# The third page of an expert's up weights, split ahead of the evacuation of the down rows

## The chip, the cores and the metric

The kernel runs on one core of one Trainium2 chip. The metric is the device time of one execution in microseconds (us); the kernel before was timed three times. Where a span of the profile is named, it is one execution under the hardware profiler, from its first to its last instruction.

## The reference, cut to what matters

The program is a decoder trunk of two layers on 1024 tokens of width 1024 (16 learned tokens stand in front). Each layer has a mixer, a layer norm, and a mixture of 32 experts of which every token uses two. All numbers are float32. For one expert, with `xb` the rows of the tokens that chose it:

```python
hb = jax.nn.silu(xb @ w_gate[e]) * (xb @ w_up[e])   # w_gate, w_up: 1024 x 512
return hb @ w_down[e]                                # w_down: 512 x 1024
```

The rows that come out are scaled by the token's gate and added to the token's row.

## The kernel before

**Pages.** The kernel keeps weights and larger tiles in 46 pages, each 128 partitions by 1040 floats. A page of weights is 512 KB. One expert needs twelve: four of gate, four of up (256 rows of the matrix each) and four of down (128 rows each). They come in the fixed order gate of expert e, down of expert e-1, up of expert e, and so on; `load_next` (L128) issues the DMA of the next page on SyncE's queue, and `pump` (L149) issues as many as the count of live pages allows.

**Splitting.** TensorE multiplies in fp32r, so each float32 operand becomes a high and a low part, and each product is three matmuls: high by high, low by high, high by low. `split` (L82 to L84) makes the two parts: ScalarE (ACT) copies the page to the high part `whi` (L83), and then VectorE (DVE) subtracts that from the page, which gives the low part `wlo` (L84). `need(i, ahead)` (L153) splits, in the fixed order, all pages up to the `ahead`-th after page `i` that are not yet split. Both parts stand in pages that a used pair has left, so a copy can wait for the last matmul that read the old pair.

**The loop over experts** (`moe`, L586 to L696). Each engine runs its instructions in the order in which this code is written. One pass, for expert e:

1. gate product of e, pages 0 to 2 (`gb`, L610 to L612);
2. the four transposes of the hidden rows of e-1 (`hpose`, tile `htr`, split to `hp`);
3. gate product, page 3;
4. down product of e-1 (`down`, tile `yb`, L644): four pages, six matmuls each, in the order `whi` four times and `wlo` twice;
5. still in `down`: ACT evacuates the two banks of `yb` into `yout`, scaled (L655), and POOL adds the rows to the output in DRAM with an indirect DMA (L657, the scatter);
6. `xpose(e + 1)`: eight transposes of the next expert's tokens (tile `tr`, L329), which ACT copies to `xh` (L83) and DVE subtracts to `xl` (L84); then POOL gathers the tokens of e+3 (L593);
7. up product of e (`ub`, L610 to L612): four pages, six matmuls each;
8. `act`: SiLU of `gb` on ACT and its product with `ub` on DVE (tile `hb`, L622 and L623).

The look-ahead is two pages (`LEAD = 2`). So the last page of down asks for the first two pages of up, and these are split before step 5. The third page of up is first asked for at step 7, by the first page of up; its copy and subtraction therefore stand behind the instructions of steps 5 and 6 on ACT and DVE.

Of the kernel before, what the change touches and what calls it, by code (L numbers as in the profile page):

```python
# [21 lines left out]
T = S + NM  # L22
KD = D // 128
NG = 4
NE = 32
# [21 lines left out]
def hybrid(ctx, tc, x, meta_tokens, lru_w_in, lru_conv_w, lru_conv_b, lru_w_a, lru_b_a, lru_w_i, lru_b_i,  # L47
# [25 lines left out]
    def free(*ts):  # L73
        live[0] -= len(ts)
# [14 lines left out]

    # ------------------------------------------------------------------ weights, in the order of their use  # L90
    items = []
# [68 lines left out]

    # ------------------------------------------------------------------ constants
    ident = cst.tile([128, 128], F32, name="ident")
# [116 lines left out]

    # ------------------------------------------------------------------ layer norm of token rows  # L280
    lnp = {}
# [32 lines left out]
    def skew(n, stages):  # L314
        """tasks: stage after stage for n tiles, each tile a step behind the one before"""
        return [(lambda st=st, i=t - st: stages[st](i)) for t in range(n + len(stages) - 1)
                for st in reversed(range(len(stages))) if 0 <= t - st < n]

    # ------------------------------------------------------------------ routing of a group of tiles
    macc = {}  # L320

    def transposes(src):
        """two banks with src^T, four blocks of 128 columns each"""
        bks = []
        for a in range(2):
            bk = bank("tr")
            for i in range(4):
                k = 4 * a + i
                PE.transpose(bk[:, 128 * i:128 * i + 128], src[:, 128 * k:128 * k + 128], ident)  # L329
            bks.append(bk)  # L330
        return bks
# [6 lines left out]
    def scr(shape, name, dt=F32, bufs=1):  # L338
        """small tile of the routing, in the buffer that the experts' rows take later"""
        n = math.prod(shape) * (2 if dt == BF else 4) // 4  # L340
        if name not in scr_at:
            scr_at[name] = (scr_top[0], n)
            scr_top[0] += n * bufs
        o, w = scr_at[name]
        assert n <= w and scr_top[0] <= D
        i = scr_n[name] = (scr_n.get(name, -1) + 1) % bufs
        ap = yout[:, o + i * w:o + i * w + n]
        if dt != F32:
            ap = ap.bitcast(dt)
        dims = "abc"[:len(shape)]  # L350
        return ap.rearrange(f"p ({' '.join(dims)}) -> p {' '.join(dims)}", **dict(zip(dims, shape)))
# [9 lines left out]
    def route_pick(l, m, pos, tiles, nrm, st):  # L361
# [22 lines left out]
        def gate_steps():  # L384
            # gates: softmax probability of the group times the softmax over the two experts
            V.tensor_scalar(rg, tg, -1.0, 1.0, op0=OP.mult, op1=OP.add)
            yield
            V.reciprocal(rg, rg)
            yield
            V.scalar_tensor_tensor(tg, tg, 1.0, rg, op0=OP.add, op1=OP.mult)  # L390
            yield
            V.tensor_reduce(sg, tg, axis=AX.X, op=OP.add)
            yield
            V.reciprocal(sg, sg)
            yield
# [45 lines left out]
    def route_send(l, m, pos, tiles, st, early, mid, late):  # L441
        # slots: rank among the tokens of the expert
        oh, ix, M = st["oh"], st["ix"], st["M"]
# [47 lines left out]

    # ------------------------------------------------------------------ experts with more than a level of tokens
    def overflow_list(l):
        """the expert and the table column of the j-th block past the first level (row j), and how many there are"""
        ps = bank("cnt")
# [88 lines left out]

    # ------------------------------------------------------------------ mixture of experts
    def moe(l, rows, comb):  # L586
# [48 lines left out]
        def down(e):  # L635
            hp = HB.pop(e)
            hh, hl = hp[:, :F], hp[:, F:2 * F]
            yb = [bank("yb") for _ in range(2)]
            for q in range(KF):
                it = need(down_it[l, e][q], min(LEAD, down_it[l, NE - 1][3] - down_it[l, e][q]))  # L640
                sl = slice(128 * q, 128 * q + 128)
                for st, w in ((hh, "h"), (hl, "h"), (hh, "l")):
                    for a in range(2):
                        PE.matmul(yb[a], st[:, sl], it[w][:, 0, 512 * a:512 * a + 512],  # L644
                                  start=q == 0 and st is hh and w == "h", stop=q == KF - 1 and w == "l")
                drop(down_it[l, e][q])
                pump(room)
            free(hp)
            if e == NE - 1:
                comb["rows"](yb)  # L650
                if not comb["rest"]:
                    return
            y = yout
            for a in range(2):
                A.activation(y[:, 512 * a:512 * a + 512], yb[a], AF.Copy, scale=tab[:, e, 2:3])  # L655
            P.memset(spacer, 0.0)
            P.indirect_dma_start(out=hsum[l], out_offset=bass.IndirectOffsetOnAxis(ap=tv[:, e, 0:1], axis=0),  # L657
                                 in_=y[:, :D], in_offset=None, bounds_check=rows - 1, oob_is_err=False,
                                 compute_op=OP.add)
            if e == NE - 1:  # L660
                comb["load"](comb["rest"])
# [35 lines left out]

    # ------------------------------------------------------------------ projection to the stream, norm, routing
    def nrow(j):
        return 2 if j == META else 128  # L700

    def router(l):
        """the norm's scale and shift move into the router's weights and bias; column sums for its mean"""
        n = NG + NE
# [20 lines left out]
    def out_proj(l, gp, its, resid, cuts, last_chunk, upto):  # L725
        """gp[j]: page of the mixer's rows of tile j, channels on partitions; resid(j, page) loads the stream's rows;
        cuts: columns that are there at the start and after each series of steps that last_chunk returns"""
        UNIT = 0.22
# [67 lines left out]
        def slots(q0, i):  # L796
            """the slot of expert 0 that each token of a tile takes, one column a slot"""
            H = scr([128], "H", BF)
# [62 lines left out]
        for bi, tiles in enumerate(BLOCKS[l]):  # L861
            last = bi == nb_ - 1
            for j in tiles:
                ys[j] = [bank("wo") for _ in range(2)]
            # the last tile takes the low parts first, then one half of the columns after the other
            for a, k in [(a, k) for a in (("l", 0, 1) if last else ("",)) for k in range(KD)]:
# [63 lines left out]

    # ------------------------------------------------------------------ norm after the experts
    def combine(l, order, seq):
        """steps for a tile: h + y / ALPHA, the last expert's rows by products; its statistics; its norm, that of
        ALPHA * h + y"""
        st, yp, oh = {}, [], []
# [75 lines left out]
        def affine(j, dst):  # L1011
            """norm, scale and shift, a half of the columns after the other"""
            for h in range(2):
# [10 lines left out]

    # ================================================================== layer 0: gated linear recurrence
    GRP = [(0, 272), (272, 656), (656, 1040)]
# [32 lines left out]
    def softplus():  # L1059
# [4 lines left out]
        P.tensor_tensor(w2, ecst, w1, op=OP.pow)  # L1064
        # log(1 + z) = 2 atanh(z / (2 + z))
        V.tensor_scalar(w1, w2, 2.0, None, op0=OP.add)
# [7 lines left out]
        V.tensor_tensor(w3, w3, w1, op=OP.mult)  # L1074
        # softplus(-lam) = max(-lam, 0) + 2 atanh(..)
        V.tensor_scalar(w1, lam, -1.0, 0.0, op0=OP.mult, op1=OP.max)
# [53 lines left out]
    def lru_decay(c, r, sp, d, q):  # L1130
        # r = (1 + th) / 2, so -log(a) = 4 softplus(-lam) (1 + th); t = tanh(-log(a) / 2)
        A.activation(d[:, :T], r[:, :T], AF.Exp, bias=sp[1][:, c:c + 1], scale=sp[1][:, c:c + 1])
        A.activation(r[:, :T], r[:, :T], AF.Tanh, bias=sp[0][:, c:c + 1], scale=sp[0][:, c:c + 1])
        # 1 / (1 + t) by a Newton step from (1 + exp(log(a))) / 2; a = 1 - 2t/(1+t), 1 - a^2 = 4t/(1+t)^2
        V.tensor_scalar(d[:, :T], d[:, :T], 0.5, 0.5, op0=OP.mult, op1=OP.add)
# [30 lines left out]
    gp = {}  # L1166
# [101 lines left out]

    # ================================================================== layer 1: gated short convolution
    GRP = [(0, 258), (258, 642), (642, 1026)]  # L1270
# [6 lines left out]
    def h_group(g, ws, bks):  # L1277
        """transposed tiles, a block of 128 columns after the other, with the products that they enter"""
        lo_, hi_ = GRP[g]
# [190 lines left out]
```

## Time and profile before

| | us |
|---|---|
| median of three runs | 2108.13 |
| lowest and highest run | 2107.02, 2109.2 |
| span of the profiled execution | 2108.8 |
| TensorE (PE), matmuls busy | 1980.4 |
| VectorE (DVE) busy | 1618.9 |
| ScalarE (ACT) busy | 1288.5 |
| GpSimd (POOL) busy | 508.3 |

The two loops over experts stand at about 420 to 1010 us and 1460 to 2055 us of the span. Times in the rows are us from the start of the span. PE is the matmuls, PEld the weight loads; SPq is SyncE's queue, which issues the loads of weights. A matmul's record is longer than the distance to the next one, since they are pipelined: the pace is the distance between starts.

### The profile page before, as it was taken

The page shows a single profiled execution, that of the slowest core. Times are in us where ns is not written, and L with a number is a line of the kernel's source. Part 1 is how long each engine was busy: PE and PEld are TensorE (multiplying, and loading weights), DVE is VectorE, ACT ScalarE, POOL GpSimd, SP SyncE. Part 2 cuts the span into 40 slices and gives each one's busy share as a digit, 9 for nine tenths or more (in the row PEclk, how much of TensorE's full clock was granted, in tenths as well). Part 3 has the DMA queues.
Part 4 walks back from the last instruction along what each step waited for, and adds up shares of the span by engine and source line. Part 5 has one row for each costly group of instructions (what it writes and reads, how often), then busy time and mean ns, then how long its engine had stood idle before and what let it go on. Part 6 is the DMA issues. An engine that isn't in the chain of part 4 may idle for free. (4 is left out here: it accounts for less than half of the span.)

```text
span 2108.8 us, 28578 instructions
## 1 busy us (share of the span) xinstructions
PE 1980.4 (94%) x10022; PEld 1677.2 (80%) x10022; DVE 1618.9 (77%) x2089; ACT 1288.5 (61%) x1640; POOL 508.3 (24%) x456
## 2 busy tenths in 40 slices
PE   8999979599999999999889999995999999999996
PEld 7999867477777877777689999873877787777773
DVE  5888875688888898888682223456898889888887
ACT  4666632288888888887630102222788888888872
POOL 3100346412221112220280001365122111222204
PEclk9999989799999999999899999997999999999998
DMA  5211455699999999996533110566999999999954
GB/s 145 57 48 41 150 190 169 248 339 357 364 352 358 353 349 352 352 357 230 166 114 106 41 51 1 200 216 239 327 360 370 368 358 361 364 356 338 365 176 185
DMA packets 255447, 520.40 MB, mean 247 GB/s; under 512 B 26755, under 2 KB 68143, under 8 KB 255300
## 3 DMA queue, kind: packets, MB, share of 16 engines
q1 hardware_dynamic: 229716, 465.31, 61.2%
q0 software_dynamic: 25584, 53.23, 8.9%
q8 instruction: 80, 1.31, 0.2%
q14 instruction: 67, 0.55, 0.1%
HBM read 492.39 MB, written 59.46 MB: 262 GB/s over the span
## 5 line engine op out<-in xcount | busy, mean ns | idle before, releaser
L84 DVE TENSOR_TENSOR wlo<-wraw,whi 128x1024 fp32r<-128x1024 f32 x810 | 955.1, 1229 | 86.8 <-ACT whi L83 74.2
L83 ACT ACTIVATE whi<-wraw 128x1024 fp32r<-128x1024 f32 x824 | 839.1, 1061 | 105.3 <-PE gb L611 34.5
L657 POOL DMA_INDIRECT hs<-yout,tab x63 | 100.0, 1587 | 935.2 <-ACT yout L655 935.2
L644 PE MATMUL yb<-whi,hp 128*128 128x512 f32 x1024 | 281.4, 396 | 1.4 <-ACT hp L83 1.4
L644 PEld LDWEIGHTS yb<-whi,hp 128*128 128x128 f32 x1024 | 193.2, 189 | 47.3 <-ACT hp L83 1.9
L612 PE MATMUL ub<-wlo,xh 128*128 128x512 f32 x512 | 208.1, 407 | 11.4 <-DVE wlo L84 11.2
L610 PE MATMUL gb<-whi,xh 128*128 128x512 f32 x512 | 207.7, 406 | 0.0
L610 PE MATMUL ub<-whi,xh 128*128 128x512 f32 x512 | 206.6, 403 | 0.0
L612 PE MATMUL gb<-wlo,xh 128*128 128x512 f32 x512 | 202.3, 395 | 2.1 <-DVE wlo L84 2.1
L611 PE MATMUL gb<-whi,xl 128*128 128x512 f32 x512 | 202.4, 395 | 0.0
L611 PE MATMUL ub<-whi,xl 128*128 128x512 f32 x512 | 201.8, 394 | 0.0
L644 PE MATMUL yb<-wlo,hp 128*128 128x512 f32 x512 | 160.9, 395 | 0.0
L84 DVE TENSOR_TENSOR xl<-tr,xh 128x512 fp32r<-128x512 f32 x128 | 82.7, 686 | 81.4 <-ACT xh L83 81.4
L612 PEld LDWEIGHTS ub<-wlo,xh 128*128 128x128 f32 x512 | 96.1, 188 | 58.0 <-DVE wlo L84 38.4
L1321 ACT ACTIVATE v<-ip 128x384 f32<-128x384 f32 (+1 forms) x24 | 9.6, 456 | 208.5 <-PE ip L1049 197.6
L84 POOL TENSOR_TENSOR wlo<-wraw,whi 128x1024 fp32r<-128x1024 f32 x14 | 39.8, 2858 | 401.6 <-ACT whi L83 401.6
L593 POOL DMA_INDIRECT xg<-hd,tab x62 | 111.3, 1795 | 38.9 <-issue 16.8
L612 PEld LDWEIGHTS gb<-wlo,xh 128*128 128x128 f32 x512 | 96.5, 188 | 25.6 <-DVE wlo L84 3.4
L644 PEld LDWEIGHTS yb<-wlo,hp 128*128 128x128 f32 x512 | 97.2, 190 | 22.8
L611 PEld LDWEIGHTS gb<-whi,xl 128*128 128x128 f32 x512 | 96.7, 189 | 20.5 <-DVE xl L84 0.9
L610 PEld LDWEIGHTS gb<-whi,xh 128*128 128x128 f32 x512 | 96.8, 189 | 20.0 <-ACT xh L83 0.5
L611 PEld LDWEIGHTS ub<-whi,xl 128*128 128x128 f32 x512 | 96.4, 188 | 19.8
(276 smaller groups left out, 3532.8 us busy)
## 6 DMA issues: line engine op xcount, KB each, us to landing
wraw<-in_moe_w_gate_dram SPq DMA_DIRECT2D x256, 512.0 KB
wraw<-in_moe_w_up_dram SPq DMA_DIRECT2D x256, 512.0 KB
wraw<-in_moe_w_down_dram SPq DMA_DIRECT2D x256, 512.0 KB
wraw<-in_sc_w_in_dram SPq DMA_DIRECT2D x24, 512.0 KB
wraw<-in_lru_w_in_dram SPq DMA_DIRECT2D x16, 512.0 KB
hy<-hs SPq DMA_DIRECT2D x16, 512.0 KB
hd<-res POOLq DMA_DIRECT2D x14, 512.0 KB
hs<-res POOLq DMA_DIRECT2D x12, 512.0 KB
```

Source lines behind the costliest of these rows:

```text
L83: A.activation(hi, src, AF.Copy)
L84: eng.tensor_tensor(lo, src, f(hi), op=OP.subtract)
L593: P.indirect_dma_start(out=xg[e % 2], out_offset=None, in_=hdr[l], in_offset=bass.IndirectOffsetOnAxis(ap=tv[:, e, 0:1], axis=0), bounds_c ...
L610: PE.matmul(bk, xh[:, sl], it["h"][:, k], start=kk == 0, stop=False)
L611: PE.matmul(bk, xl[:, sl], it["h"][:, k], start=False, stop=False)
L612: PE.matmul(bk, xh[:, sl], it["l"][:, k], start=False, stop=kk == KD - 1)
L644: PE.matmul(yb[a], st[:, sl], it[w][:, 0, 512 * a:512 * a + 512], start=q == 0 and st is hh and w == "h", stop=q == KF - 1 and w == "l")
L657: P.indirect_dma_start(out=hsum[l], out_offset=bass.IndirectOffsetOnAxis(ap=tv[:, e, 0:1], axis=0), in_=y[:, :D], in_offset=None, bounds_c ...
L1321: A.activation(zt[c][:, a:b], bk[:, :b - a], AF.Copy)
```

## The change

Two lines are added in `down`, between the last matmul of the down product and the evacuation:

```diff
                 drop(down_it[l, e][q])
                 pump(room)
             free(hp)
+            if e + 1 < NE:
+                need(up_it[l, e + 1][2], 0)
             if e == NE - 1:
                 comb["rows"](yb)
```

Here `e` is the expert of the down product, so `e + 1` is the expert whose up product follows. The rest of the diff takes comments out. On TensorE, SyncE and POOL the instructions stand in the same order as before.

On ACT, in one pass of the first layer: `wraw_5903` and `wraw_5951` are the first and second page of up, `wraw_5963` the third, `wraw_5975` the fourth, `wraw_5991` and `wraw_5993` the next expert's first gate pages. Before:

```order
L83 ACTIVATE whi_6445<-wraw_5951 128x1024
L655 ACTIVATE yout_99<-yb_6407,tab_121 128x512
L655 ACTIVATE yout_99<-yb_6408,tab_121 128x512
L83 ACTIVATE xh_6463<-tr_6465 128x512
L83 ACTIVATE xh_6463<-tr_6470 128x512
L83 ACTIVATE whi_6483<-wraw_5963 128x1024
L83 ACTIVATE whi_6493<-wraw_5975 128x1024
```

And of the changed kernel, at the same place:

```order
L83 ACTIVATE whi_6445<-wraw_5951 128x1024
L83 ACTIVATE whi_6457<-wraw_5963 128x1024
L657 ACTIVATE yout_99<-yb_6407,tab_121 128x512
L657 ACTIVATE yout_99<-yb_6408,tab_121 128x512
L83 ACTIVATE xh_6467<-tr_6469 128x512
L83 ACTIVATE xh_6467<-tr_6474 128x512
L83 ACTIVATE whi_6493<-wraw_5975 128x1024
```

The third page's copy has moved from behind the four instructions of steps 5 and 6 to ahead of them; the fourth page's copy stands where it stood.

On DVE, in the same pass, before:

```order
L84 TENSOR_TENSOR wlo_6446<-wraw_5951,whi_6445 128x1024
L84 TENSOR_TENSOR xl_6464<-tr_6465,xh_6463 128x512
L84 TENSOR_TENSOR xl_6464<-tr_6470,xh_6463 128x512
L84 TENSOR_TENSOR wlo_6484<-wraw_5963,whi_6483 128x1024
L84 TENSOR_TENSOR wlo_6494<-wraw_5975,whi_6493 128x1024
```

And of the changed kernel:

```order
L84 TENSOR_TENSOR wlo_6446<-wraw_5951,whi_6445 128x1024
L84 TENSOR_TENSOR wlo_6458<-wraw_5963,whi_6457 128x1024
L84 TENSOR_TENSOR xl_6468<-tr_6469,xh_6467 128x512
L84 TENSOR_TENSOR xl_6468<-tr_6474,xh_6467 128x512
L84 TENSOR_TENSOR wlo_6494<-wraw_5975,whi_6493 128x1024
```

The subtraction of the third page has moved ahead of the two of the next tokens. The move on ACT stands at 62 places of the program (31 passes in each layer), that on DVE at 60, since the last pass of a layer has no next tokens.

## Rows read from the trace of the kernel before

**Rows 1.** Busy time by stretch, about one pass of the loop; columns first.

```profile
core 0: us, PE busy (x) PEld busy (x) DVE busy (x) ACT busy (x) POOL busy (x), PEclk, DMA share, GB/s
700.00:718.44 18.44, 18.26 (x87) 14.67 (x85) 16.56 (x16) 15.25 (x19) 3.60 (x3) 1.00 1.00 355
```

**Rows 2.** Waits of TensorE over the span: total, times, longest.

```profile
PE ub L612 <- DVE wlo L84: 11.2, 60, 0.2
```

**Rows 3.** Timeline of TensorE, one pass: start, duration, line, idle before.

```profile
714.79 1.09 PE L644 MATMUL yb<-whi,hp 128*128 128x512 f32 x4
...
716.18 1.09 PE L644 MATMUL yb<-whi,hp 128*128 128x512 f32 x4
717.11 0.62 PE L644 MATMUL yb<-wlo,hp 128*128 128x512 f32 x2
...
718.36 0.48 PE L610 MATMUL ub<-whi,xh 128*128 128x512 f32 x1
...
722.04 0.50 PE L612 MATMUL ub<-wlo,xh 128*128 128x512 f32 x1 [0.18 <-DVE wlo L84]
...
724.23 0.39 PE L612 MATMUL ub<-wlo,xh 128*128 128x512 f32 x1
```

**Rows 4.** Timeline of TensorE, the first expert's up product.

```profile
423.14 0.47 PE L610 MATMUL ub<-whi,xh 128*128 128x512 f32 x1
...
426.46 0.39 PE L612 MATMUL ub<-wlo,xh 128*128 128x512 f32 x1
...
427.85 0.39 PE L612 MATMUL ub<-wlo,xh 128*128 128x512 f32 x1
...
428.55 0.39 PE L612 MATMUL ub<-wlo,xh 128*128 128x512 f32 x1
```

**Rows 5.** Timeline of ACT in the pass of rows 3.

```profile
715.92 1.06 ACT L83 ACTIVATE whi<-wraw 128x1024 fp32r<-128x1024 f32 x1 [0.33 <-PE yb L644]
717.54 1.26 ACT L655 ACTIVATE yout<-yb,tab 128x512 f32<-128x512 f32 x2 [0.56 <-PE yb L644]
718.70 1.08 ACT L83 ACTIVATE xh<-tr 128x512 fp32r<-128x512 f32 x2
719.65 2.97 ACT L83 ACTIVATE whi<-wraw 128x1024 fp32r<-128x1024 f32 x3
```

**Rows 6.** Timeline of DVE in the same pass.

```profile
712.38 5.85 DVE L84 TENSOR_TENSOR wlo<-wraw,whi 128x1024 fp32r<-128x1024 f32 x5 [0.25 <-ACT whi L83]
719.33 1.29 DVE L84 TENSOR_TENSOR xl<-tr,xh 128x512 fp32r<-128x512 f32 x2 [1.09 <-ACT xh L83]
720.76 4.63 DVE L84 TENSOR_TENSOR wlo<-wraw,whi 128x1024 fp32r<-128x1024 f32 x4
725.31 0.68 DVE L623 TENSOR_TENSOR hb<-hb,ub 128x512 f32<-128x512 f32 x1
725.91 1.22 DVE L84 TENSOR_TENSOR wlo<-wraw,whi 128x1024 fp32r<-128x1024 f32 x1
```

**Rows 7.** Timeline of POOL, two passes.

```profile
700.63 1.59 POOL L657 DMA_INDIRECT hs<-yout,tab  x1 [14.55 <-ACT yout L655]
...
719.09 1.58 POOL L657 DMA_INDIRECT hs<-yout,tab  x1 [14.55 <-ACT yout L655]
720.97 1.92 POOL L593 DMA_INDIRECT xg<-hd,tab  x1 [0.31 <-issue]
```

**Rows 8.** Waits of ACT for a load, first layer's loop: total, times, longest.

```profile
ACT whi L83 <- DMA wraw<-in_moe_w_gate_dram: 0.3, 1, 0.3
```

**Rows 9.** Timeline of SyncE's queue, last loads of the first layer's experts.

```profile
967.72 4.11 SPq L133 DMA_DIRECT2D wraw<-in_moe_w_down_dram  x4
```

**Rows 10.** Busy time by stretch behind these loads, columns as in rows 1.

```profile
970.00:975.00 5.00, 5.00 (x23) 4.11 (x22) 4.67 (x6) 4.83 (x6) 0.00 (x0) 1.00 0.96 371
975.00:980.00 5.00, 5.00 (x27) 4.16 (x27) 3.72 (x5) 3.81 (x6) 1.61 (x2) 1.00 0.40 135
```

**Rows 11.** Timeline of ACT, last copies of the first layer's experts.

```profile
1003.35 4.84 ACT L83 ACTIVATE whi<-wraw 128x1024 fp32r<-128x1024 f32 x5
```

## The prediction

> **What bounds the kernel now.** I read the busy time by stretch first. In a pass of the loop over experts TensorE (PE) is busy 18.26 of 18.44 us at the full granted clock (1.00, that is 2.4 GHz), while DVE has 16.56 and ACT 15.25 [rows 1]. So PE sets the pace of the pass, and only what lets it stop is worth time. The scatter, once a pass, comes every 719.09 - 700.63 = 18.46 us [rows 7]. The DMA share in the same stretch is 1.00 [rows 1], which makes the loads a second candidate; I come back to it among the rivals.
>
> Next the waits of PE. In the loop there is one that repeats: the up product's low-part matmul (L612) waits for DVE's `wlo`, 60 times, 11.2 us in all [rows 2]. That total is the idle time between records whose ends are modelled, so I measure what it costs by starts instead. The first expert of a layer has no down product before its up product, and its 24 matmuls run without a stop: the 15th starts 426.46 - 423.14 = 3.32 us after the first, the 21st 4.71, the last 5.41 [rows 4]. In the pass of rows 3 the 15th, which is the first to read the third page's low part, starts 722.04 - 718.36 = 3.68 after the first, so 0.36 late, and the last 5.87 after it, so 0.46 late. The stop costs 0.46 us a pass: 0.36 of waiting and 0.10 lost on starting again.
>
> Then the timelines of ACT and DVE, to see why the low part is late. ACT evacuates the down rows from 717.54, copies the next tokens from 718.70, and only at 719.65 begins the third page [rows 5]. DVE stands idle for 1.09 us until the tokens' copy is there, does the two subtractions, and starts the third page's at 720.76 [rows 6]; the matmul starts 1.28 later, at 722.04 [rows 3].
>
> **The change, part by part.** It adds and removes no instruction; it moves one copy on ACT (62 places) and one subtraction on DVE (60 places) ahead of the evacuation and the tokens. PE, SyncE and POOL keep their order, and no load is issued earlier or later in any queue.
>
> *When the third page's copy starts.* It needs two free pages. In the kernel before, the second page's copy waits for PE: it starts at 715.92 [rows 5], 0.04 after the four `whi` matmuls of the last but one down page (714.79 + 1.09 = 715.88) [rows 3]. The next copy in the order takes the pair freed next, that of the last down page, whose `whi` matmuls end at 716.18 + 1.09 = 717.27; so it starts at 717.31. From below: ACT itself is free at 715.92 + 1.06 = 716.98. From above: the whole down product ends at 717.11 + 0.62 = 717.73. I take 717.31, which follows the nearest row.
>
> *What ACT then does.* Copies in a row follow each other by (2.97 - 1.06) / 2 = 0.955 [rows 5], so the evacuation starts at 718.27, 0.73 later than now. The tokens follow after 718.70 - 717.54 = 1.16, at 719.43, and the fourth page after another 0.95, at 720.38.
>
> *What DVE does.* A subtraction starts 720.76 - 719.65 = 1.11 after its copy [rows 5, 6]. The third page's runs from 718.42, when DVE is free (712.38 + 5.85 = 718.23), to 719.64 (1.22 each): in the time in which DVE idles now. The matmul could use it at 718.42 + 1.28 = 719.70 and wants it at 718.36 + 3.32 = 721.68, so it is 2 us early. The tokens' subtractions start 0.63 after their copy as now (719.33 - 718.70), at 720.06, and end at 721.35.
>
> *What is late next.* The fourth page: subtraction at 720.38 + 1.11 = 721.49, usable at 722.77, wanted by the 21st matmul at 718.36 + 4.71 = 723.07. That is 0.30 early. With the copy's bounds above it is 0.63 early or 0.12 late. Behind it DVE goes on without a gap, 1.14 a page ((4.63 - 1.22) / 3): first gate page 722.63, second 723.77, the product `hb` 724.91, third gate page 0.60 later at 725.51 and usable at 726.79. PE, 0.46 earlier than now, starts the next gate product at 724.00 and wants that page 14 steps of 0.233 later, at 727.26: 0.47 early. None of the later pages is tighter, since four transposes and ACT's own waits for PE come between.
>
> *What the moved work holds up.* The evacuation is 0.73 later and the scatter behind it too; POOL is idle for 14.55 us before each scatter [rows 7], so nothing queues there. The copied tokens are first read by the next gate product at 724.0, over 2 us after 721.35. The two banks of the down rows come free 0.73 later, when PE is in the middle of the up product and takes no new bank. I cost these at nothing.
>
> *Sum.* 60 passes by 0.46 us = 27.6 us. The last pass of each layer has no tokens to copy and only a shorter stop; I leave it out. From the profiled span of 2108.8 that gives 2081.2. The median of the runs shown is 0.7 below that span, so I predict 2080.5.
>
> **The rivals.**
>
> *A. The wait moves to the fourth page.* Its reserve of 0.30 is the smallest in the sum. With the copy at its upper bound the matmul is 0.12 late and pays 0.10 for starting again: 0.22 of the 0.46 come back, 13.2 us in 60 passes, and the time is about 2094. At 0.36 late nothing is gained. Against it: the second page's copy starts, in the kernel before, with the last `whi` matmul of the pair that it takes over, and not with the end of a product [rows 3, 5].
>
> *B. The loads cannot follow.* The DMA share is 1.00 at 355 GB/s [rows 1]; a pass of 17.98 us would want 355 x 18.46 / 17.98 = 364. If that can't be had, PE lives on the stock of pages loaded ahead. Over a layer it would draw 30 x 0.46 = 13.8 us more from it. The stock at the end can be read: the last four down pages are issued from 967.72 to 971.83 [rows 9], and the DMA share falls from 0.96 to 0.40 between 970 and 980 [rows 10], so all have landed before 980. The last two of them are copied from 1003.35 on [rows 11], 23 us later. 13.8 fit into 23, and ACT waited for a load once, 0.3 us [rows 8]. Were the stock empty, the time would stay at 2108.
>
> *C. Slower: the gather comes to stand against the fourth page's subtraction.* POOL's queue slides by 0.73: the gather runs from 721.70 to 723.62 instead of from 720.97 [rows 7], and the fourth page's subtraction is now its neighbour. If DVE had to wait until the gather is done, the fourth page would be usable at 723.62 + 1.28 = 724.90, 1.83 late, a pass would lose 1.93 in place of 0.46, and 60 passes 88 us: about 2196. It decides as soon as the subtraction starts later than 721.49 + 0.30 + 0.36 = 722.15. Against it: now the gather runs from 720.97 to 722.89 beside the first two of four subtractions, which take 4.63 / 4 = 1.16 each, and the five with no POOL beside them take 5.85 / 5 = 1.17 [rows 6, 7]. By the Trainium skill (SBUF — State Buffer, section "SBUF: two separate sides") GpSimd and a VectorE operation with two SBUF inputs can lock each other out of a shared port for a whole instruction; the rows just named show no such lock for this pair of instructions, so I give the rule little.
>
> *D. Another wait takes the whole place*, 0.36 or more, of a kind that these rows do not show: no change, 2108.
>
> **How the numbers follow.** The forecast 0.76, A 0.10, B 0.06, D 0.03, C 0.05. About 0.2% (4.2 us) is what a measurement of this kernel can tell from no change. The forecast, A and half of B are faster by more than that: 0.89; D and the other half of B are the same: 0.06; C is slower: 0.05. The forecast's own range is 2077 to 2085: 0.05 us a pass either way in the cost of the stop, and the run-to-run spread. The range runs on upward to take in A's worked case: 2077 to 2096.
>
> **What would show it.** In the changed kernel's waits of PE the line of the up product for `wlo` is gone or a few entries long. In the timeline the last matmul of an up product starts 5.4 us after its first, not 5.87, and scatters follow each other by 18.0 us. On ACT the copy of the third page starts about 0.2 before the down product ends, and the evacuation starts about 0.7 after it. DVE's idle 1.09 us before the tokens shrinks to about 0.4. A wait at the 21st matmul would be A; waits of ACT's copies for loads late in a layer would be B; subtractions of over 1.3 us beside the gather would be C. The prediction is wrong if the stop at the 15th matmul goes and the pass is still over 18.3 us long.

## The result, and the profile after

| | before | after |
|---|---|---|
| median of the runs, us | 2108.66 (2107.02 to 2110.83, 4 runs) | 2077.29 (2075.48 to 2079.23, 4 runs) |
| span of the profiled execution | 2108.8 | 2073.7 |
| start of the first up product of layer 1 | 423.14 | 418.99 |
| from there to the start of the last up product of layer 2 | 1629.77 | 1601.30 |
| from there to the end of the span | 55.9 | 53.4 |

The changed kernel takes 0.9853 of the time before (95% interval 0.9841 to 0.9865): 31.4 us less, where 27.6 were forecast. That is inside the range of 2077 to 2096, but by 0.3 us only. The wait of [rows 2] is gone: this is all that the up and gate products wait for in the whole span. Columns are total, times, longest.

```profile
PE gb L612 <- DVE wlo L84: 1.2, 2, 0.8
```

By stretch, the pass that answers to [rows 1] is 17.98 us long, as is the one behind it, and TensorE (PE) is busy in all of it.

```profile
core 0: us, PE busy (x) PEld busy (x) DVE busy (x) ACT busy (x) POOL busy (x), PEclk, DMA share, GB/s
689.37:707.35 17.98, 17.98 (x88) 14.77 (x86) 16.60 (x16) 15.32 (x20) 3.59 (x3) 1.00 0.99 351
707.35:725.33 17.98, 17.98 (x88) 14.79 (x86) 16.60 (x17) 15.32 (x20) 3.59 (x3) 1.00 0.97 349
```

The timeline of PE in the second of these passes, the first row being the `whi` matmuls of the last but one down page:

```profile
703.80 1.08 PE L644 MATMUL yb<-whi,hp 128*128 128x512 f32 x4
...
705.17 1.09 PE L644 MATMUL yb<-whi,hp 128*128 128x512 f32 x4
706.10 0.62 PE L644 MATMUL yb<-wlo,hp 128*128 128x512 f32 x2
707.35 0.48 PE L610 MATMUL ub<-whi,xh 128*128 128x512 f32 x1
...
710.65 0.39 PE L612 MATMUL ub<-wlo,xh 128*128 128x512 f32 x1
...
712.04 0.40 PE L612 MATMUL ub<-wlo,xh 128*128 128x512 f32 x1
...
712.74 0.39 PE L612 MATMUL ub<-wlo,xh 128*128 128x512 f32 x1
712.97 0.40 PE L610 MATMUL gb<-whi,xh 128*128 128x512 f32 x1
```

The 15th matmul of the up product starts 3.30 us after the first, the 21st 4.69 and the last 5.39: the figures of the undisturbed product of [rows 4] (3.32, 4.71, 5.41) and not those of [rows 3]. ACT and DVE in the same pass answer to [rows 5, 6]:

```profile
704.91 1.07 ACT L83 ACTIVATE whi<-wraw 128x1024 fp32r<-128x1024 f32 x1 [0.33 <-PE yb L644]
706.29 1.06 ACT L83 ACTIVATE whi<-wraw 128x1024 fp32r<-128x1024 f32 x1 [0.31 <-PE yb L644]
707.26 1.25 ACT L657 ACTIVATE yout<-yb,tab 128x512 f32<-128x512 f32 x2
708.40 1.09 ACT L83 ACTIVATE xh<-tr 128x512 fp32r<-128x512 f32 x2
709.36 2.02 ACT L83 ACTIVATE whi<-wraw 128x1024 fp32r<-128x1024 f32 x2
```

```profile
701.44 7.17 DVE L84 TENSOR_TENSOR wlo<-wraw,whi 128x1024 fp32r<-128x1024 f32 x6 [0.26 <-ACT whi L83]
709.03 1.29 DVE L84 TENSOR_TENSOR xl<-tr,xh 128x512 fp32r<-128x512 f32 x2 [0.42 <-ACT xh L83]
710.47 3.50 DVE L84 TENSOR_TENSOR wlo<-wraw,whi 128x1024 fp32r<-128x1024 f32 x3
713.88 0.68 DVE L623 TENSOR_TENSOR hb<-hb,ub 128x512 f32<-128x512 f32 x1
```

The third page's copy is the one at 706.29. Its subtraction is the sixth of the group that begins at 701.44 (before there were five), and stands in what was DVE's idle time, of which 0.42 is left. The group at 710.47 begins with the fourth page.

### The profile page after: what moved, and what is told of

It reads as the page before. It is cut to its first block, busy times and chain, and to the rows that moved or that the text cites. A ratio compares the mean times of both kernels' runs of the same rounds, so it can differ in the third digit from the quotient of the medians.

```text
span 2073.7 us, 28630 instructions
## 1 busy us (share of the span) xinstructions
PE 1958.9 (94%) x10022; PEld 1677.6 (81%) x10022; DVE 1623.4 (78%) x2089; ACT 1289.0 (62%) x1640; POOL 510.4 (25%) x456
## 5 line engine op out<-in xcount | busy, mean ns | idle before, releaser
L612 PE MATMUL ub<-wlo,xh 128*128 128x512 f32 x512 | 201.4, 393 | 0.0
L610 PEld LDWEIGHTS ub<-whi,xh 128*128 128x128 f32 x512 | 96.3, 188 | 19.7
```

Of the source, the lines that this page charges most:

```text
L610: PE.matmul(bk, xh[:, sl], it["h"][:, k], start=kk == 0, stop=False)
L612: PE.matmul(bk, xh[:, sl], it["l"][:, k], start=False, stop=kk == KD - 1)
```

## The experiments

### What belongs to the change: the same programs again, and marked

Both kernels ran once more, and each again with one needless instruction on POOL, in the second layer only, and so later in the program than all that stands ahead of the first loop:

```diff
             P.memset(spacer, 0.0)
+            if l == 1:
+                P.memset(spacer, 0.0)
             P.indirect_dma_start(out=hsum[l], ...
```

> The changed kernel once more, unchanged. My theory: all of the change's gain is 0.46 us in each of the passes of the two loops over experts (about 28 us), and the 4.15 us by which the profiled run was ahead before the first pass began is the scatter of that unchanged part from run to run. Expected: 2077 us (2075 to 2080), up product 5.4 us long, passes 18.0 us, and a first up product that starts anywhere between 418 and 424 us of the span. Rival: the change also shortens the part before the loops; then the first up product starts at about 419 us again and in every kernel that holds the change.

> The kernel before once more, under the profiler, to see whether the 4 us by which the changed kernel is ahead at the start of the first expert's up product (418.99 against 423.14) belong to the kernel or to the single execution. Theory 1, it belongs to the program as a whole (it repeats when the same program runs again, but is set by something that shifts with any edit): first up product at 422.8 to 423.5, first to last up product 1629.8 within 0.5, time 2108. Rival, it varies from one execution to the next: anywhere from 418 to 424. Rival, the change itself gives the 4 us: 423.1 too, so this run alone does not tell it from theory 1; the next two do.

> The kernel before with one needless instruction added: in the second layer POOL clears its one-element spacer twice ahead of each scatter instead of once (0.09 us on an engine that idles 14.5 us there). Up to the second layer the program is word for word the same. Theory 1: the loops stay at 5.87 us an up product and 1629.8 within 1 from first to last, while the first up product can start anywhere from 418 to 424 and not at 423.1; time 2103 to 2110. Rival, what stands ahead of the loops decides by itself: 423.1 within 0.4 again.

> The changed kernel with the same needless instruction on POOL in the second layer. Theory 1: up products 5.41 us, 1601.3 within 0.6 from first to last, the first at anywhere from 418 to 424; time 2073 to 2081. Rival, the change itself makes the part ahead of the loops shorter: 418.9 within 0.4. In either case the difference between this kernel and the one before it in this list, taken from first to last up product, is 28.5.

The three times of a row, in us, are of one profiled execution; the ratio compares medians of several runs with the kernel before. First up product is its start; first to last is from there to the start of the last up product; behind is from there to the end.

| | first up product | first to last | behind | ratio (95%) |
|---|---|---|---|---|
| before | 423.14 | 1629.77 | 55.9 | |
| before again | 422.06 | 1629.98 | 55.8 | 0.9999 (0.9989 to 1.0009) |
| before, marked | 419.30 | 1629.84 | 55.9 | 0.9996 (0.9986 to 1.0005) |
| after | 418.99 | 1601.30 | 53.4 | 0.9853 (0.9841 to 0.9865) |
| after again | 418.91 | 1601.24 | 53.4 | 0.9856 (0.9839 to 0.9872) |
| after, marked | 422.11 | 1601.17 | 53.4 | 0.984 (0.9823 to 0.9856) |

What follows: the 4 us ahead of the loops do not belong to the change. With the mark the kernel before starts its first up product at 419.30 and the changed kernel at 422.11, the other way round. My theory that this start is fixed for one program did not hold well either: the kernel before moved by 1.1 when it ran again. Two parts do belong to the change, and repeat within 0.3: 28.5 us in the loops, and 2.5 behind them. Together they are 31.0, of a measured 31.4.

### The last expert of all

The 2.5 us behind the loops were not in my sum. To find their place, the change was made at one place of its 62:

```diff
-            if e + 1 < NE:
+            if e + 2 == NE and l == 1:
                 need(up_it[l, e + 1][2], 0)
```

> Only one of the 62 places is changed: the third page is split early ahead of the very last expert's up product, in the second layer; everywhere else the code is that of the kernel before. From the start of the last up product to the end of the span the kernel before takes 55.9 us and the changed kernel 53.4. Theory: these 2.5 us come from that one place. There the shorter DVE queue lets the product of the hidden rows start 0.93 earlier behind the last up product, TensorE stands idle before the four transposes 0.85 us instead of 1.41, and its granted clock then does not fall in the last down product, which takes 5.9 us instead of 7.5. So 53.4 here, with the loops at 1629.8 as in the kernel before, and a time 2.5 below it. Rival: the clock's fall at the end depends on the stops in the passes before, so that it comes here as in the kernel before: 0.93 earlier but 7.5 for the down product, 55.0, time 0.9 below the kernel before. Second rival: the tail varies from kernel to kernel: 55.9.

Measured: 53.4 behind the last up product, ratio 0.9989 (0.9980 to 0.9999). The place is the right one. The passes of the loops are as long as before, but first to last is 1630.65, 0.7 to 0.9 more than in the kernel before, 0.8 of it between the two loops; so the median is 1.6 lower and not 2.5. PE behind the last up product, in the kernel before (run again) and then in this one, from the transposes of the hidden rows on:

```profile
2059.54 0.65 PE L630 MATMUL htr<-ident,hb 128*128 128x128 f32 x4 [1.42 <-DVE hb L623]
2060.88 1.95 PE L644 MATMUL yb<-whi,hp 128*128 128x512 f32 x4 [0.69 <-ACT hp L83]
2062.63 1.05 PE L644 MATMUL yb<-wlo,hp 128*128 128x512 f32 x2
2063.48 1.77 PE L644 MATMUL yb<-whi,hp 128*128 128x512 f32 x4
```

```profile
2058.08 0.66 PE L630 MATMUL htr<-ident,hb 128*128 128x128 f32 x4 [0.85 <-DVE hb L623]
2059.42 1.45 PE L644 MATMUL yb<-whi,hp 128*128 128x512 f32 x4 [0.69 <-ACT hp L83]
2060.71 0.63 PE L644 MATMUL yb<-wlo,hp 128*128 128x512 f32 x2
2061.18 1.09 PE L644 MATMUL yb<-whi,hp 128*128 128x512 f32 x4
```

Six matmuls take 63.48 - 60.88 = 2.60 us in the first and 61.18 - 59.42 = 1.76 in the second. The granted clock of the 5 us that begin 8.80 after the start of the last up product, first of the one and then of the other (the column behind POOL's):

```profile
2060.84:2065.84 5.00, 4.96 (x14) 3.69 (x15) 3.05 (x3) 1.88 (x2) 0.00 (x0) 0.66 0.96 354
```

```profile
2060.29:2065.29 5.00, 5.00 (x22) 4.09 (x23) 2.36 (x2) 0.97 (x2) 0.00 (x0) 1.00 0.95 324
```

In the last pass DVE's product of the hidden rows stands behind the subtractions, and PE has nothing else to do. One subtraction less in that queue starts the transposes 0.91 earlier, counted from the last up product, after 0.85 instead of 1.42 us of idleness. Here the clock then does not fall from 2.4 to 1.2 GHz for part of the down product, which saves another 1.5. That the shorter idleness keeps it up fits all kernels of this record, but it is not the whole rule, as the last section shows.

### One layer only

```diff
-            if e + 1 < NE:
+            if e + 1 < NE and l == 1:
                 need(up_it[l, e + 1][2], 0)
```

> The change in the second layer's loop alone. Theory (a stop of 0.46 us goes in each pass and nothing else changes): half of the gain, 14 us off the kernel before, about 2094 us (2091 to 2097); up products 5.87 us long in the first layer and 5.4 in the second. Rival (part of the gain arises outside the passes, at the layers' ends or before them): a time more than 4 us away from the middle between the kernel before and the changed one.

Measured: 2092.33, ratio 0.9929 (0.9913 to 0.9946). Up products take 5.87 in the first layer and 5.41 in the second; first to last is 1615.71, the middle between 1629.8 and 1601.3. The gain is a sum of passes.

### The place and the whole step

Two kernels ask whether the place matters, and whether the ACT half of the step alone would do. The first puts the two lines of the change between the evacuation and the tokens:

```diff
             for a in range(2):
                 A.activation(y[:, 512 * a:512 * a + 512], yb[a], ...)
+            if e + 1 < NE:
+                need(up_it[l, e + 1][2], 0)
```

> The third page is split between the evacuation and the next tokens, no longer ahead of both. Theory (it is the idle time of DVE while it waits for the tokens that must be used, and ACT must serve the copy early enough for it): ACT copies the page at 718.70 and the tokens from 719.65; DVE subtracts the page from 719.81, the tokens from 720.95 to 722.24, and only then the fourth page, usable at 723.5, while TensorE wants it at 723.07. The stop moves to the 21st matmul, 0.46 late and 0.10 for the restart: 60 x 0.56 = 34 us over the changed kernel, about 2111 us (2104 to 2117). Rival (any place ahead of the tokens does): 2077 us and no stop.

Measured: 2105.85, ratio 0.9992 (0.9982 to 1.0002). No gain; the wait has moved to the fourth page. DVE, the third page first, and PE, the first and the 21st matmul of the same up product:

```profile
718.31 1.23 DVE L84 TENSOR_TENSOR wlo<-wraw,whi 128x1024 fp32r<-128x1024 f32 x1 [1.55 <-PE ub L611]
719.45 1.28 DVE L84 TENSOR_TENSOR xl<-tr,xh 128x512 fp32r<-128x512 f32 x2
720.65 3.49 DVE L84 TENSOR_TENSOR wlo<-wraw,whi 128x1024 fp32r<-128x1024 f32 x3
```

```profile
716.89 0.48 PE L610 MATMUL ub<-whi,xh 128*128 128x512 f32 x1
...
721.92 0.50 PE L612 MATMUL ub<-wlo,xh 128*128 128x512 f32 x1
722.26 0.40 PE L610 MATMUL ub<-whi,xh 128*128 128x512 f32 x1
```

DVE still idles ahead of the third page, 1.55 us, and then has four subtractions in a row; the fourth page's starts at 720.65, the 21st matmul needs it at 716.89 + 4.69 = 721.58 and starts at 721.92: 0.34 late, and 0.11 more lost at the next (0.34 to it instead of 0.23). I had expected a longer stop, 0.46, by reckoning DVE's steps too long.

The second moves only the copy on ACT, and leaves the subtraction behind the tokens:

```diff
+            if e + 1 < NE:
+                split_next(V, HELD)      # ACT's copy alone
...
+                split_rest(HELD)         # DVE's subtraction
                 ub = bank("ub")
                 proj(e, up_it[l, e], ub)
```

> One part of the change alone: ACT's copy of the third page stands ahead of the evacuation, DVE's subtraction stays behind those of the tokens. Theory: the copy pushes the tokens 0.73 us back on ACT, DVE waits for them, subtracts them from 720.06 to 721.35 and the third page after that, usable at 722.66 where 721.68 is wanted: 0.98 late and 0.10 for the restart, at the 15th matmul. 60 x 1.08 = 65 us over the changed kernel: about 2142 us (2134 to 2150), slower than the kernel before. Rival (the earlier copy is what pays, since the subtraction waited for it): between 2077 and 2095 us.

Measured: 2130.15, ratio 1.0109 (1.0093 to 1.0126): slower than the kernel before, as expected, but by less than the 2134 to 2150 that I had written down. An up product takes 6.34 us, 0.93 more than in the changed kernel, where 1.08 was reckoned.

```profile
724.52 1.29 DVE L84 TENSOR_TENSOR xl<-tr,xh 128x512 fp32r<-128x512 f32 x2 [1.81 <-ACT xh L83]
725.73 1.21 DVE L153 TENSOR_TENSOR wlo<-wraw,whi 128x1024 fp32r<-128x1024 f32 x1
```

```profile
727.00 0.50 PE L621 MATMUL ub<-wlo,xh 128*128 128x512 f32 x1 [0.64 <-DVE wlo L153]
```

The copy delays the tokens, DVE idles 1.81 us for them, and the third page's low part comes behind them. So the gain is not in the early copy: it is in the subtraction that fills DVE's idle time.

### How large the reserve at the fourth page is

The prediction's nearest rival hung on a reserve of 0.30 us at the 21st matmul. Two kernels spend it: one evacuates the first bank a second time, the other both banks.

```diff
-            for a in range(2):
+            for a in (0, 0, 1):       # the other kernel: (0, 1, 0, 1)
                 A.activation(y[:, 512 * a:512 * a + 512], yb[a], ...)
```

> The changed kernel with the first bank of the down rows evacuated twice: ACT has one more instruction of 0.59 us ahead of the tokens and of the fourth page. It measures the reserve of the fourth page (0.30 us by my sum). Theory: the fourth page is 0.29 late and the restart costs 0.10: 0.39 us in 60 passes, 23 us over the changed kernel, about 2100 us (2094 to 2105), with the stop at the 21st matmul. Rival (the reserve is larger than 0.6 us, or ACT has slack there): 2077 us.

> The changed kernel with both banks of the down rows evacuated twice: two more instructions, about 1.13 us, ahead of the tokens and of the fourth page on ACT. Theory: the fourth page is 0.83 late, and with the restart 0.93 us are lost in 60 passes: 56 us over the changed kernel, about 2133 us (2126 to 2140). From one bank to both the time grows by 0.54 us a pass, one for one with ACT's added work. Rival (ACT has slack there): under 2100 us.

Measured: 2108.83, ratio 1.0002 (0.9993 to 1.0012), for one bank: a miss, since 2094 to 2105 was expected; 2135.92, ratio 1.0130 (1.0113 to 1.0147), for both. ACT with one bank twice, then the 21st matmul with one bank and with both:

```profile
719.40 1.97 ACT L657 ACTIVATE yout<-yb,tab 128x512 f32<-128x512 f32 x3
721.26 1.08 ACT L83 ACTIVATE xh<-tr 128x512 fp32r<-128x512 f32 x2
```

```profile
724.61 0.50 PE L612 MATMUL ub<-wlo,xh 128*128 128x512 f32 x1 [0.25 <-DVE wlo L84]
```

```profile
729.71 0.50 PE L612 MATMUL ub<-wlo,xh 128*128 128x512 f32 x1 [0.53 <-DVE wlo L84]
```

The tokens' copy starts 721.26 - 719.40 = 1.86 after the evacuation instead of 1.14, so one more evacuation costs ACT 0.72; I had taken 0.59. The up product of the first begins at 719.50, so its 21st matmul is 724.61 - 719.50 - 4.69 = 0.42 late: 0.72 - 0.42 leaves 0.30. In the second the fourth page's subtraction is 1.15 later than in the changed kernel, the up product begins at 724.16, and the matmul is 729.71 - 724.16 - 4.69 = 0.86 late: 1.15 - 0.86 leaves 0.29. The reserve is what the prediction made it; the miss was the price of the added instruction. That price belongs to one bank evacuated twice in a row: with both banks twice, ACT's four evacuations take 726.35 - 724.07 = 2.28 us where two take 1.14, so 0.57 for each that was added.

```profile
724.07 2.40 ACT L657 ACTIVATE yout<-yb,tab 128x512 f32<-128x512 f32 x4
726.35 1.11 ACT L83 ACTIVATE xh<-tr 128x512 fp32r<-128x512 f32 x2
```

Past the reserve, ACT's time lands on PE one for one, and the restart of 0.1 comes on top.

### The fourth page too

```diff
-                need(up_it[l, e + 1][2], 0)
+                need(up_it[l, e + 1][3], 0)
```

> The fourth page of up is split ahead of the evacuation too. Theory (TensorE has no stop left in the up product, so the pass is at its matmuls' own pace): the same as the changed kernel, 2077 us (2074 to 2081), with passes of 18.0 us. Rival (each page split earlier takes some of the pass away): 28 us less, about 2050 us. Rival (the evacuation and the tokens, now 1.7 us later than at first, become the wait): a stop at the next gate product and over 2085 us.

Measured: 2081.37, ratio 0.9874 (0.9857 to 0.9890), 0.4 above the range that I had written down. First to last up product is 1601.25, as in the changed kernel: with no stop left, more reserve gives nothing there. Its execution under the profiler is longer ahead of the loops (421.52) and behind them (56.6). The second belongs to the edit. DVE and POOL at the last scatter:

```profile
2024.41 3.49 DVE L84 TENSOR_TENSOR wlo<-wraw,whi 128x1024 fp32r<-128x1024 f32 x3
```

```profile
2024.67 4.67 POOL L659 DMA_INDIRECT hs<-yout,tab  x1 [15.50 <-ACT yout L657]
```

The scatter starts during the first of three subtractions, and takes 4.67 us where it takes 1.59 in the changed kernel; it ends 1.44 after the last of them (2029.34 - 2027.90). At the end of the first layer it takes 4.66 in the same way. The rows that it writes are loaded back next: that load is issued 11.7 us after the start of the last up product, in place of 8.0 in the changed kernel, the load of the last norm's scale stands behind it, and DVE's first product with that scale starts 3.4 later. So more reserve gave nothing in the loop and cost about 3 us at the end.

### The stock of loads

The page count up to which loads are issued ahead was cut:

```diff
-        room = NPAGES - 4
+        room = NPAGES - 16
```

> The changed kernel with twelve pages fewer for loads ahead (room of 30 live pages in place of 42). In the changed kernel the loads, from issue to copy, are 54 us ahead early in the first layer and 14 us at its end, since 12 pages take the DMA queues about 19.3 us and TensorE 18.0. Theory: with about 19 us less of stock the first layer's loop runs dry some passes before its end and then goes at the loads' pace, about 11 us lost there and 2 in the second layer: about 2090 us (2083 to 2100), copies that wait for loads in the last passes of the first layer and not in its first. Rival (the loads keep pace and the stock is not needed): 2077 us. Rival (the room sets how far ahead the splits run, and the early passes suffer as well): over 2105 us.

Measured: 2090.32, ratio 0.9914 (0.9897 to 0.9930). Passes are 18.0 us long until 800 us, then 18.7 to 19.7 up to the layer's last; in the second layer only the last passes are longer. Busy time at the start and near the end of the first layer's loop, and ACT's waits for loads, none of which is earlier than 750 us:

```profile
430.00:600.00 170.00, 170.00 (x795) 139.22 (x794) 156.08 (x152) 139.40 (x171) 32.35 (x27) 1.00 0.98 348
...
880.00:965.00 85.00, 82.04 (x372) 63.78 (x370) 76.28 (x78) 67.32 (x80) 15.81 (x15) 1.00 0.99 355
```

```profile
ACT whi L83 <- DMA wraw<-in_moe_w_down_dram: 12.4, 19, 1.5
ACT whi L83 <- DMA wraw<-in_moe_w_up_dram: 7.1, 28, 0.3
```

So the changed kernel lives on its stock, as rival B had it, and two fifths of the gain (13.0 of 31.4) are lost where that is too small. In the changed kernel itself it lasts: the DMA share falls from 0.99 to 0.60 at 975 to 980 us, and the last down pages are copied in the group from 984.05 on, 4 to 9 us later (23 by [rows 9 to 11]; 23 - 13.8 = 9 was reckoned).

```profile
970.00:975.00 5.00, 5.00 (x23) 4.04 (x22) 4.59 (x5) 5.00 (x7) 0.00 (x0) 1.00 0.99 373
975.00:980.00 5.00, 5.00 (x24) 4.05 (x23) 4.45 (x5) 4.49 (x6) 1.61 (x2) 1.00 0.60 187
```

```profile
984.05 4.84 ACT L83 ACTIVATE whi<-wraw 128x1024 fp32r<-128x1024 f32 x5
```

## Why the prediction was right, and what it left out

**When the third page's copy starts: right.** 706.29, 0.03 after the pair's `whi` matmuls end (705.17 + 1.09); the bounds on either side were not needed.

**What ACT and DVE then do: right.** Counted from the first up matmul, in us, forecast and measured:

| | forecast | measured |
|---|---|---|
| evacuation starts | -0.09 | -0.09 |
| tokens' copy | 1.07 | 1.05 |
| fourth page's copy | 2.02 | 2.01 |
| tokens' subtraction | 1.70 | 1.68 |
| fourth page's subtraction | 3.13 | 3.12 |
| next gate product | 5.64 | 5.62 |
| product `hb` | 6.55 | 6.53 |

**What is late next: nothing, by 0.3 us.** The two kernels with a longer evacuation measured that reserve, and rival A with it; the kernel with the step behind the evacuation is rival A in the flesh.

**The sum: mechanism right, one term left out.** 60 passes by 0.46 = 27.6 was forecast for the loops; 28.5 was measured. 56 of the passes gave 0.45 each (25.4) and the last one counted in each layer 0.4. The one before that gave 1.0 in each layer: there the gate product waits for its low part too, 0.3 us in the first layer and 1.4 in the second, and in the changed kernel 0 and 0.8. The step that failed is "a shorter stop; I leave it out": in the second layer that last pass was worth 2.5 us, 0.9 by the earlier transposes and 1.6 by the clock, since PE has no other work there. 28.5 + 2.5 = 31.0 agrees with the 31.4 of the medians. The range had no room for this term below: that the median fell 0.3 inside it is luck, and two of the four runs, 2075.48 and 2076.13, lie under it.

The last pass of the first layer shows the same: the transposes start 0.9 earlier, and the down product takes 5.69 us from its first matmul to its last in place of 7.26. But at the first up product of the second layer only 0.15 of it is left. The clock stood lower in between: 0.83 in place of 0.89 in the 30 us that begin 385 us after the last up product, and 0.63 in place of 0.67 in the 41 us ahead of the second loop's first up product. That this took back the rest is likely, not shown. What moves the start of the loops between 418.3 and 423.4 from one execution and one program to another stays open; the runs show only that it isn't the change.

**The rivals.** B was real but had room, as reckoned. D did not appear. C did not either: the gather runs beside the fourth page's subtraction now,

```profile
708.79 1.58 POOL L659 DMA_INDIRECT hs<-yout,tab  x1 [14.05 <-ACT yout L657]
710.68 1.92 POOL L593 DMA_INDIRECT xg<-hd,tab  x1 [0.31 <-PE ub L612]
```

and the three subtractions from 710.47 on take 3.50 / 3 = 1.17 us each, as the five with no POOL beside them in [rows 6] (5.85 / 5). So DVE does not wait for POOL. That these rows show no lock at all was a wrong reading in the prediction, though: POOL waits for DVE. The gather's 1.92 us, here and in [rows 7], are not its own time. In the kernel with the step behind the evacuation it starts beside the tokens' subtractions (from 719.45), which read one of their two inputs from PSUM, and takes 1.03:

```profile
719.50 1.03 POOL L593 DMA_INDIRECT xg<-hd,tab  x1 [0.31 <-issue]
```

A page's subtraction has both inputs in SBUF. Where the gather starts 0.21 behind the start of one, it takes 1.92, and with the copy alone, 0.44 behind (726.17 and 725.73), 1.68; each time it ends 0.91 after that subtraction. The Trainium skill (SBUF — State Buffer, section "SBUF: two separate sides") tells of a lock between a GpSimd operation that reads SBUF and a VectorE operation with two SBUF inputs: whichever starts first has the shared ports for its whole instruction. These runs agree where the subtraction is first. They do not show it the other way: the subtraction that starts during the gather is not held up. In the loop this costs nothing, since POOL idles for 14 us before each scatter.

## What to carry to other kernels

When an engine that runs in order stands idle ahead of a wait and is late just behind it, move into the gap a whole step that is ready, with both of its halves: half the step (the copy alone) or the step one place later cost time or gave nothing, because the gap then stayed. Measure a stop by the distance between starts against an undisturbed instance of the same loop body, look for the next late consumer, and reckon its reserve before the gain. And don't leave out the last pass: where the bottleneck engine has no other work, the same change can be worth several times what it is in the loop, 2.5 us here against 0.46.

## What the runs showed of the hardware

**The clock hangs on a short idleness, and not on that alone.** In the last pass of the second layer PE idles before the transposes, then 0.69 us before the down product. In the five kernels with 1.41 to 1.67 us there whose clock fell (before, before again, before marked, one bank twice, both banks twice) the 5 us behind showed 0.66; in the eight with 0.85 it stayed at 1.00. But with the step behind the evacuation the idleness was 1.40, and the clock stayed at 1.00 too:

```profile
2059.53 0.66 PE L630 MATMUL htr<-ident,hb 128*128 128x128 f32 x4 [1.40 <-DVE hb L623]
```

```profile
2060.83:2065.83 5.00, 4.96 (x20) 3.78 (x21) 3.05 (x3) 1.88 (x2) 0.00 (x0) 1.00 0.96 359
```

That kernel also shows what the clock alone is worth: its transposes start as late as in the kernel before, and behind the last up product it takes 54.3 us, 1.6 less than that kernel and 0.9 more than the changed one. At the end of the first layer 1.41 us stood before the fall in the kernel before, and before none with one bank twice and with the last expert alone. So 1.4 us can go either way. By the Trainium skill (TensorE: Matmul & The Clock Gate, "Part 1: The HAM clock gate") what watches PE's activity runs freely and is not reset when a kernel starts. If so, the same gap can fall well or badly; these runs agree with that but don't prove it.

**A stop costs more than its wait.** The matmul behind one that waited starts 0.33 to 0.34 after it instead of 0.23, wherever the stop was put: 0.10 to 0.11 each time.

**A gather or scatter on POOL waits for a subtraction that is running.** The gather takes 1.03 us beside the tokens' subtractions and 1.92 or 1.68 where one of a page has just started; the scatter takes 1.59 and, beside three subtractions in a row, 4.67. The subtractions beside it take 1.17 us as ever.
